# Seven products for eight on both pairs of output blocks of the down-projection, in four of its five portions

## The chip, the cores and the metric

The kernel runs on one core of one Trainium2 chip. The metric is the device time of one execution in microseconds (us): 2098.43 us is the median of three runs before the change (2096.87 to 2099.15). The core has a matrix engine (TensorE, PE in the profile, with PEld for loading its stationary operand), VectorE (DVE), ScalarE (ACT), GpSimd (POOL) and SyncE (SP), which here issues loads from HBM. Each engine works through its own list of instructions in order and waits on semaphores for the others.

## The reference

An encoder of two layers on 256 tokens of width 2048, in float32. Cut to what matters:

```python
for l in range(DEPTH):                      # DEPTH = 2
    h = rms_norm(x, ln1_g[l])
    qa, ka, va, qb, kb, vb = split(h @ w_in[l])
    oa = neighborhood_attention(...)        # 8 heads of 128, 2-D window
    ob = windowed_gqa_sink(...)             # 8 query heads, 2 key heads, band of +-128
    o = concatenate([rms_norm(oa, on_a[l]), rms_norm(ob, on_b[l])])
    x = x + o @ w_out[l]
    h2 = rms_norm(x, ln2_g[l])
    u = depthwise_conv(h2 @ w_up[l], conv_w[l], conv_b[l])   # 2048 -> 2 x 5632
    gate, up = u[..., :5632], u[..., 5632:]
    x = x + (silu(gate) * up) @ w_down[l]                    # 5632 -> 2048
```

The change concerns the last two lines, above all the product with w_down.

## The kernel before

**Precision.** Every weight that is multiplied is split into a rounded high part (ScalarE, line 114, tile `whi`) and the remainder (VectorE, line 115, tile `wlo`), 1024 columns at a time; activations are split in the same way. A product is then three matmuls: high by high, low by high, high by low. All of them are recorded under line 100, the helper `mm`.

**Quanta and steps.** The program is a list of quanta. A quantum is one load of 1024 KB of weights (tile `raw`, three buffers, issued on SP's queue at line 749 when the last split of the quantum three places earlier is done) and the matmuls that use it. It consists of two steps (three for a seven-product quantum, "seven"). While step s multiplies, the weights of step s + 4 are split (`SPLIT_AHEAD`), into five buffers each of `whi` and `wlo`. In every second quantum of an up block, the low part of the second half is not made by VectorE: seven steps ahead (`EARLY`) ScalarE writes the negated rounded weights into `v_a` or `v_b` (line 775), and a DMA on POOL's queue adds the raw weights to them (line 776). Which step is done so is decided by `by_transfer`.

**The feed-forward part.** The 5632 hidden columns are 44 blocks of 128. An up block f is two quanta, 64 matmuls; it accumulates in a PSUM tile "mm", of which there are two (two banks each), and `glu` (lines 544 to 570) reads it: a copy on ScalarE (548), an addition on VectorE (549) that is the last to read PSUM, the convolution (550 to 560), the gate (562, 564), and a split into the middle operand `mid`, which the down-projection uses as its stationary operand.

The down-projection goes in five portions (`CHUNKS`) of 8, 8, 8, 8 and 12 blocks. The 2048 output columns are four blocks of 512. For the first two of them, and pairs of hidden blocks, the four products of two token halves, two hidden blocks and two output blocks are done as seven products (a Strassen-like scheme) over four pairs: six of the seven in a seven-product quantum (`q_seven`, 18 matmuls of 512 columns in three steps), the seventh for all four pairs together in one "plain" quantum (`q_plain`, 12 matmuls). It needs sums of middle operands (`sums_mid`, once for every pair of blocks) and sums of weights, which VectorE forms in `raw` (lines 755 to 757, within `split_seven`). Six accumulators are open from the first of the four quanta to the last: one "mm" tile for two of them, both tiles "S", and "tr" and "pv". At the end `add_seven` adds them into `x` (lines 620 to 628). The last two output blocks go by ordinary quanta (`q_down`, 24 matmuls each), added to x on line 484.

**Order.** It is written out by hand at the end of `encoder_kernel`. In each layer nine up blocks come first; then each of the first four portions is: plain, four times a seven-product and an ordinary quantum, and eight up blocks of the next portion. The fifth portion is: plain, then seven-product quanta with the three remaining up blocks between them, then eight ordinary quanta. Splits of weights and `add_seven` have a higher scheduling priority than the rest (`AHEAD_PRIO`).

**Tiles.** Middle operands and operand sums are all tiles of the same size under the name "mid", 17 of them (`MIDS`); three further ones in the last portion use "qT" (`SPARE`), a tile of attention that is idle by then.

## Time and profile before

| what | value |
|---|---|
| median of the runs shown (range) | 2098.43 us (2096.87 to 2099.15) |
| the profiled execution | 2098.86 us |
| its span, first to last instruction | 2097.1 us |
| granted TensorE clock | 1.000 |
| weights read from HBM | 404.42 MB |

The profile is of one execution. A busy time is the time in which at least one instruction of the engine ran; a mean is the duration of one instruction, and neighbours overlap, so that means add up to more than busy time. Idle time is put down to the instruction or transfer that ended it ("<-"). Numbers such as L549 are lines of the kernel. The chain is followed back from the last instruction to whatever released each.

### The profile page before, as it was taken

How to read it: one execution, taken by the hardware profiler on the slowest of the kernel's cores; microseconds unless marked ns; L12 is line 12 of the kernel's file. 1: busy time of each engine (PE TensorE's matmuls, PEld its weight loads, DVE VectorE, ACT ScalarE, POOL GpSimd, SP SyncE). 2: the span in 40 equal slices, each digit the busy share in tenths (PEclk: the TensorE clock that was granted, in tenths of full speed). 3: DMA queues.
4: the chain of work that ended last, by engine and by line, in shares of the span. 5: the costliest groups of instructions: out<-in, count | busy, mean ns of one | idle time of the engine just before them, and what ended most of it. 6: DMA issues, size and time to landing. Idle time of an engine off the chain costs nothing.

```text
span 2097.1 us, 29473 instructions
## 1 busy us (share of the span) xinstructions
PE 2086.1 (99%) x10816; PEld 1787.8 (85%) x10816; DVE 1623.0 (77%) x2516; ACT 1308.8 (62%) x1905; POOL 241.5 (12%) x325
## 2 busy tenths in 40 slices
PE   9999999999999999999999999999999999999999
PEld 8888888888888888888888888888888888888887
DVE  7786656797887978788857766667978879788786
ACT  7566556766666666576555665567666666666663
POOL 0011101101101011020000111011011110111100
PEclk9999999999999999999999999999999999999999
DMA  9544557858678586787555455578686785867864
GB/s 351 196 145 166 175 181 213 242 204 252 206 253 267 206 258 201 229 272 230 208 181 181 161 169 171 165 220 248 209 256 206 243 254 210 270 199 240 262 211 161
DMA packets 74817, 454.57 MB, mean 217 GB/s; under 512 B 8752, under 2 KB 11312, under 8 KB 26416
## 3 DMA queue, kind: packets, MB, share of 16 engines
q1 hardware_dynamic: 61280, 405.46, 54.4%
q0 software_dynamic: 12672, 46.14, 12.3%
q8 instruction: 85, 1.39, 0.3%
q10 hardware_dynamic: 720, 1.08, 0.2%
q14 instruction: 60, 0.49, 0.1%
HBM read 404.42 MB, written 2.10 MB: 194 GB/s over the span
## 4 chain that ended last, share of the span: by engine, by line
PE 95%; DVE 2%; DMA 1%; issue 1%; ACT 1%; ACTq 0%; DVEq 0%; SPq 0%
PE mm L100 86%; PE S L100 3%; PE pv L100 2%; PE tr L100 1%; DVE wlo L115 1%; PE tr L375 1%; ACT whi L114 1%; PE tr L309 1%; PE S L151 0%; DMA v_a<-raw 0%; DMA mid<-in_xT 0%; DMA raw<-in_w_seven 0%; DMA raw<-in_w_up 0%; DVE pT L560 0%; DVE prob L549 0%
## 5 line engine op out<-in xcount | busy, mean ns | idle before, releaser
L115 DVE TENSOR_TENSOR wlo<-raw,whi 128x1024 fp32r<-128x1024 f32 (+1 forms) x709 | 858.2, 1221 | 298.2 <-ACT whi L114 265.8
L114 ACT ACTIVATE whi<-raw 128x1024 fp32r<-128x1024 f32 (+1 forms) x709 | 736.4, 1053 | 449.9 <-PE mm L100 220.7
L100 PE MATMUL mm<-xs,whi 128*128 128x512 f32 x2816 | 977.0, 390 | 3.0 <-DVE prob L549 3.0
L100 PEld LDWEIGHTS mm<-xs,whi 128*128 128x128 f32 x2816 | 527.8, 188 | 113.9 <-DVE prob L549 3.9
L100 PE MATMUL mm<-xs,wlo 128*128 128x256 f32 x2112 | 596.4, 282 | 0.6 <-DVE wlo L115 0.6
L100 PEld LDWEIGHTS mm<-xs,wlo 128*128 128x128 f32 x2112 | 399.1, 189 | 2.6 <-DVE wlo L115 1.5
L100 PE MATMUL mm<-whi,mid 128*128 128x512 f32 x1412 | 369.9, 392 | 1.6 <-DVE prob L549 1.2
L100 PEld LDWEIGHTS mm<-whi,mid 128*128 128x128 f32 x1412 | 262.5, 188 | 56.6 <-DVE prob L549 2.1
L100 PE MATMUL mm<-whi,xs 128*128 128x512 f32 x1152 | 294.7, 393 | 0.4 <-ACT whi L114 0.4
L100 PEld LDWEIGHTS mm<-whi,xs 128*128 128x128 f32 x1152 | 212.7, 188 | 43.1 <-ACT whi L114 1.4
L100 PE MATMUL mm<-wlo,mid 128*128 128x512 f32 x706 | 201.9, 392 | 0.0
L100 PE MATMUL mm<-wlo,xs 128*128 128x512 f32 x576 | 158.8, 392 | 0.0
L100 PEld LDWEIGHTS mm<-wlo,mid 128*128 128x128 f32 x706 | 132.2, 188 | 27.4
L560 DVE SCALAR_TENSOR_TENSOR pT<-halo,conv,pT 128x256 f32<-128x256 f32 x352 | 148.7, 481 | 6.5 <-ACT pT L558 1.6
L100 PEld LDWEIGHTS mm<-wlo,xs 128*128 128x128 f32 x576 | 107.0, 188 | 21.5
L552 POOL COPY halo<-halo 128x6 f32<-128x6 f32 x88 | 78.4, 891 | 352.8 <-DVE halo L550 352.8
L788 ACT ACTIVATE whi<-raw 128x1024 fp32r<-128x1024 f32 x88 | 92.7, 1053 | 40.1 <-PE mm L100 40.1
L558 ACT ACTIVATE pT<-halo,conv 128x256 f32<-128x256 f32 x176 | 96.0, 592 | 23.2 <-DVE halo L550 21.1
L100 PE MATMUL mm<-xs,v_a 128*128 128x256 f32 x352 | 99.3, 282 | 0.0
L100 PE MATMUL mm<-xs,v_b 128*128 128x256 f32 x352 | 99.2, 282 | 0.0
L776 POOL DMA_DIRECT2D v_b<-raw x44 | 38.1, 866 | 524.1 <-ACT v_b L775 299.6
L549 DVE TENSOR_TENSOR prob<-prob,mm 128x512 f32<-128x512 f32 x88 | 60.3, 685 | 46.9 <-ACT prob L548 46.9
(189 smaller groups left out, 1922.5 us busy)
## 6 DMA issues: line engine op xcount, KB each, us to landing
raw<-in_w_up SPq DMA_DIRECT2D x176, 1024.0 KB, 5.7
raw<-in_w_in SPq DMA_DIRECT2D x71, 1024.0 KB, 4.9
raw<-in_w_down SPq DMA_DIRECT2D x48, 1024.0 KB, 4.9
raw<-in_w_seven SPq DMA_DIRECT2D x40, 1024.0 KB, 5.1
raw<-in_w_out SPq DMA_DIRECT2D x32, 1024.0 KB, 4.8
v_a<-raw POOLq DMA_DIRECT2D x44, 512.0 KB, 5.5
v_b<-raw POOLq DMA_DIRECT2D x44, 512.0 KB, 5.1
raw<-in_w_plain SPq DMA_DIRECT2D x10, 1024.0 KB, 4.9
```

What stands on the lines that cost most here:

```text
L100: nc.tensor.matmul(ps, lhsT, rhs, start=start, stop=stop, skip_group_check=True)
L114: high = nc.scalar.activation(hi, src, AF.Copy)
L115: nc.vector.tensor_sub(lo, src, hi.bitcast(F32))
L309: nc.tensor.transpose(ps[:, j, tt * P:(tt + 1) * P], qn[tt][:, p + j, :], ident)
L375: nc.tensor.transpose(ps[:, kt, tt * P:(tt + 1) * P], p[:, tt, kt * P:(kt + 1) * P], ident)
L549: nc.vector.tensor_add(t, t, ps[:, :, 1])
L552: nc.gpsimd.tensor_copy(ux[:, :, 1:r], ux[:, :, T:T + r - 1])
L558: nc.scalar.activation(y[:, j, :], ux[:, j, r:r + T], AF.Identity, scale=w1, bias=b)
L560: nc.vector.scalar_tensor_tensor(y[:, j, :], ux[:, j, o:o + T], w, y[:, j, :], op0=ALU.mult, op1=ALU.add)
L776: nc.gpsimd.dma_start(out=lo, in_=src, accum_op=ALU.add)
L788: highs[s] = nc.scalar.activation(hl[s][0], raw[q][:, half * 1024:(half + 1) * 1024], AF.Copy)
```

## The change

- In the first four portions both pairs of output blocks go by seven products. `w_seven` and `w_plain` have one more index m for the pair, and `q_seven`, `q_plain` and `add_seven` take it. `q_down` remains for the fifth portion's second pair and remainder.
- The order in these portions is new: for each pair m a group of seven-product quantum 0, plain, seven-product 1, up, seven-product 2, up, seven-product 3, up, up. The eight up blocks of a portion thus stand within its two groups, and none is left ahead of the next portion.
- The operands of a portion live until its second group has used them. `middle` takes a tile from a table of names, MIDDLE: 17 "mid", and 3 "qT", 3 "qtok", 2 "kT" and 1 "kTb" of attention; `drop` gives a pair's names back.
- The second half of a plain quantum also has its low part made by ScalarE and a DMA.
- A few tiles have other widths (`ro`, `v_b`), and an 8-column tile `pad` is new.

```diff
@@ -53,7 +53,7 @@
 UP_AT = 56
 WARM = 14
 
-SPARE = 3 * (("qT", 3),)
+MIDDLE = (("mid", MIDS), ("qT", 3), ("qtok", 3), ("kT", 2), ("kTb", 1))
 
 EARLY = 7
 
@@ -171,7 +171,7 @@
         ps = psum.tile([P, TT], F32, name="pv", bufs=1)
         for tt in range(TT):
             mm(ps[:, tt:tt + 1], acc_o[grp][:, tt * P:(tt + 1) * P], ones[:, 0:1], True, True)
-        st["ro"] = act.tile([P, 16], F32, name="ro", bufs=2)[:, 0:TT]
+        st["ro"] = act.tile([P, TT], F32, name="ro", bufs=2)
         rsqrt(ps, 1.0 / (NH * HD), st["ro"], "c2")
 
 
@@ -267,6 +267,8 @@
 
     def evac_qk(ps, nh, kind):
 
+        if "pad" not in par:
+            par["pad"] = work.tile([P, 8], F32, name="pad", bufs=1)
         n = nh * HD
         grp, isq = kind[1], kind[0] == "q"
         qn = []
@@ -516,16 +518,23 @@
             at(q + 1, stat_x, which)
 
     gs = {}
-    count = {}
+    free, kept = {}, {}
 
     def middle(l, f):
 
-        name, bufs = "mid", MIDS
-        if f >= NF - CHUNKS[-1]:
-            k = count[l] = count.get(l, 0) + 1
-            if k > MIDS:
-                name, bufs = SPARE[k - MIDS - 1]
-        return act.tile([P, 2, T], F32R, name=name, bufs=bufs)
+        if f == 0 and l not in kept:
+            free.clear()
+            free.update(MIDDLE)
+            kept[l] = {}
+        name = max(free, key=lambda n: (free[n] > 0, n == "mid", free[n]))
+        assert free[name] > 0
+        free[name] -= 1
+        kept[l].setdefault(f // 2, []).append(name)
+        return (work if name == "qtok" else act).tile([P, 2, T], F32R, name=name, bufs=dict(MIDDLE)[name])
+
+    def drop(l, p):
+        for name in kept[l].pop(p):
+            free[name] += 1
 
     def q_up(l, f, u):
         def body(q, half, hi, lo):
@@ -584,7 +593,7 @@
             for j in range(2):
                 ss[p, 2 * i + j] = t[:, :, j * P:(j + 1) * P]
 
-    def q_seven(l, c, i):
+    def q_seven(l, c, m, i):
 
         f = sum(CHUNKS[:c]) + 2 * i
         p = f // 2
@@ -606,16 +615,20 @@
                 for x_part, w in ((0, hv), (1, hv), (0, lv)):
                     mm(ps[n], x2[:, x_part], w[:, j], i == 0 and x_part == 0 and w is hv,
                        i == PAIRS - 1 and w is lv)
-            if i == PAIRS - 1 and part == 2:
-                with tc.high_priority(offset=AHEAD_PRIO):
-                    add_seven(ps)
+            if part == 2:
+                if m == 1 and i > 0:
+                    drop(l, p)
+                if i == PAIRS - 1:
+                    with tc.high_priority(offset=AHEAD_PRIO):
+                        add_seven(m, ps)
         return body
 
-    def add_seven(ps):
+    def add_seven(m, ps):
 
         t = work.tile([P, 4, HD], F32, name="tq", bufs=2).rearrange("p a d -> p (a d)")
-        x11, x12 = x[:, 0, 0:512], x[:, 0, 512:1024]
-        x21, x_2, x2_ = x[:, 1, 0:512], x[:, :, 512:1024], x[:, 1, 0:1024].rearrange("p (j n) -> p j n", j=2)
+        xm = x[:, :, m * 1024:(m + 1) * 1024]
+        x11, x12 = xm[:, 0, 0:512], xm[:, 0, 512:1024]
+        x21, x_2, x2_ = xm[:, 1, 0:512], xm[:, :, 512:1024], xm[:, 1, 0:1024].rearrange("p (j n) -> p j n", j=2)
         both = lambda v: v[:, None, :].to_broadcast([P, 2, 512])
         nc.vector.tensor_add(x11, x11, ps[1])
         nc.scalar.activation(t, ps[1], AF.Copy)
@@ -639,7 +652,7 @@
             for tt in range(TT):
                 nc.sync.dma_start(out=out[:, tt, m], in_=x[:, tt, m])
 
-    def q_plain(l, c):
+    def q_plain(l, c, m):
 
         f0 = sum(CHUNKS[:c])
 
@@ -653,8 +666,10 @@
                     mm(ps, gs[f0 + 4 * half + 2 * i + 1][:, x_part, 0:P], w[:, i],
                        half == 0 and i == 0 and x_part == 0 and w is hv, half == 1 and i == 1 and w is lv)
             if half == 1:
-                xv = x[:, 0, 0:512]
+                xv = x[:, 0, m * 1024:m * 1024 + 512]
                 nc.vector.tensor_add(xv, xv, ps)
+                if m == 1:
+                    drop(l, f0 // 2)
         return body
 
     def q_down(l, c, nb, g):
@@ -711,18 +726,22 @@
         for c, nf in enumerate(CHUNKS):
             up = lambda f: [(a["w_up"][l, f, u], q_up(l, f, u), "up") for u in range(2)]
             down = lambda nb, g: [(a["w_down"][l, sum(CHUNKS[:c]) // FG + g, nb], q_down(l, c, nb, g), "")]
-            seven = lambda i: [(a["w_seven"][l, c, i], q_seven(l, c, i), "seven")]
-
-            end = sum(CHUNKS[:c]) + PART + 1
-            while f < end:
+            seven = lambda i, m=0: [(a["w_seven"][l, c, m, i], q_seven(l, c, m, i), "seven")]
+            plain = lambda m=0: [(a["w_plain"][l, c, m], q_plain(l, c, m), "plain")]
+
+            while f < PART + 1:
                 quanta += up(f)
                 f += 1
-            quanta.append((a["w_plain"][l, c], q_plain(l, c), ""))
             if nf == PART:
-                for i in range(PAIRS):
-                    quanta += seven(i) + down(2 + i // 2, i % 2)
+                for m in range(2):
+                    quanta += seven(0, m) + plain(m)
+                    for i in range(1, PAIRS + 1):
+                        if i < PAIRS:
+                            quanta += seven(i, m)
+                        quanta += up(f)
+                        f += 1
             else:
-
+                quanta += plain()
                 for i in range(PAIRS):
                     quanta += seven(i)
                     if f < NF:
@@ -762,14 +781,15 @@
 
     def by_transfer(s):
         q, half = steps[s]
-        return quanta[q][2] == "up" and half == 1 and last_up[q]
+        return half == 1 and (quanta[q][2] == "plain" or last_up.get(q, False))
 
     def low_w(s):
 
         if s < len(steps) and by_transfer(s):
             q, half = steps[s]
             src = raw[q][:, half * 1024:(half + 1) * 1024]
-            lo = lows[s] = act.tile([P, 1024], F32R, name=("v_a", "v_b")[turns[0] % 2], bufs=1)
+            n = turns[0] % 2
+            lo = lows[s] = act.tile([P, 1024 + 8 * n], F32R, name=("v_a", "v_b")[n], bufs=1)[:, 0:1024]
             turns[0] += 1
             with tc.high_priority(offset=AHEAD_PRIO):
                 nc.scalar.activation(lo, src, AF.Copy, scale=-1.0)
@@ -943,10 +963,10 @@
     wd = f["w_down"]
     n = NF // PART
 
-    four = wd[:, :n * PART * P, :1024].reshape(L, n, PART // 2, 2, P, 2, 512)
-    o["w_seven"] = c(np.stack([four[:, :, :, k, :, m] for k, m in ((1, 0), (1, 1), (0, 1), (0, 0))], 4)).reshape(
-        L, n, PART // 2, P, 2048)
-    o["w_plain"] = c(four[:, :, :, 1, :, 0].transpose(0, 1, 3, 2, 4)).reshape(L, n, P, 2048)
+    four = wd[:, :n * PART * P].reshape(L, n, PART // 2, 2, P, 2, 2, 512).transpose(0, 1, 5, 2, 3, 4, 6, 7)
+    o["w_seven"] = c(np.stack([four[:, :, :, :, k, :, m] for k, m in ((1, 0), (1, 1), (0, 1), (0, 0))], 5)).reshape(
+        L, n, 2, PART // 2, P, 2048)
+    o["w_plain"] = c(four[:, :, :, :, 1, :, 0].transpose(0, 1, 2, 4, 3, 5)).reshape(L, n, 2, P, 2048)
     o["w_down"] = c(f["w_down"].reshape(L, NF // FG, FG, P, NB, 512).transpose(0, 1, 4, 3, 2, 5)).reshape(
         L, NF // FG, NB, P, 2048)
```

## The prediction

> **What bounds the kernel now.** I read the engine totals and the chain that ended last first, then the chain in order of time, then windows over single stages.
>
> ```profile
> span 2097.1 us, 29473 instructions
> PE 2086.1 (99%) x10816; PEld 1787.8 (85%) x10816; DVE 1623.0 (77%) x2516; ACT 1308.8 (62%) x1905; POOL 241.5 (12%) x325
> PE 95%; DVE 2%; DMA 1%; issue 1%; ACT 1%; ACTq 0%; DVEq 0%; SPq 0%
> ```
>
> ```profile
> 467.27 94.69 PE mm L100 x538
> 596.86 94.69 PE mm L100 x538
> 726.46 94.69 PE mm L100 x538
> 856.05 84.21 PE mm L100 x480
> ...
> 1030.47 5.45 PE mm L100 x24
> ```
>
> TensorE (PE) is 95% of the chain. The chain repeats itself every 129.59 us (467.27, 596.86, 726.46, 856.05): that is one of the portions that the change edits, eight blocks of the up-projection ("ups") and then the down-projection of eight blocks. The last row gives the pace: 24 matmuls of 512 columns in 5.45 us, 0.227 us each. A "busy" mean of 390 ns for the same matmul counts overlapped time and is not used.
>
> ```profile
> core 0: us, PE busy (x) PEld busy (x) DVE busy (x) ACT busy (x) POOL busy (x), PEclk, DMA share, GB/s
> 467.27:596.86 129.59, 129.59 (x693) 112.44 (x693) 108.58 (x158) 84.12 (x111) 16.45 (x24) 1.00 0.74 235
> 856.05:944.30 88.25, 88.25 (x505) 77.94 (x505) 67.56 (x109) 59.20 (x82) 15.37 (x22) 1.00 0.84 256
> 948.52:1004.39 55.87, 53.08 (x279) 44.93 (x277) 45.53 (x62) 36.51 (x48) 3.60 (x9) 1.00 0.65 210
> 1993.25:2048.39 55.14, 53.08 (x278) 44.91 (x276) 45.65 (x62) 36.32 (x48) 3.61 (x9) 1.00 0.66 213
> 556.99:596.87 39.88, 39.88 (x182) 33.20 (x181) 39.56 (x48) 24.28 (x29) 1.17 (x2) 1.00 0.53 186
> ```
>
> In that portion PE has no gap, while VectorE (DVE) is busy 108.58 of 129.59 us. Eight ups take 88.25 us, 11.03 each. The two rows from 948.52 and from 1993.25 are the one place where the kernel already does what the change does everywhere: the fifth portion's first stretch, a plain product, then four seven-product steps with three ups between them. Only there does PE lose time: its work is 3 x 11.03 + (12 + 4 x 18) x 0.227 = 52.16 us, and it takes 55.87 and 55.14, a loss of 3.71 and 2.98.
>
> ```profile
> 956.10 0.38 PE L100 MATMUL mm<-xs,wlo 128*128 128x256 f32 x1 [0.37 <-DVE wlo L115]
> 988.27 0.50 PE L100 MATMUL mm<-xs,whi 128*128 128x512 f32 x1 [1.75 <-DVE prob L549]
> 1004.39 0.50 PE L100 MATMUL mm<-whi,mid 128*128 128x512 f32 x1 [0.67 <-DVE prob L549]
> 981.75 1.06 ACT L775 ACTIVATE v_b<-raw 128x1024 fp32r<-128x1024 f32 x1 [2.94 <-DMA raw<-in_w_up]
> 983.78 1.23 DVE L115 TENSOR_TENSOR wlo<-raw,whi 128x1024 fp32r<-128x1024 f32 x1 [2.99 <-ACT whi L114]
> ```
>
> How that loss arises: a load of weights is late by 2.94 us for ScalarE (ACT) at 981.75; DVE, which subtracts ACT's rounded part from the weights, idles 2.99 us behind it; DVE's addition on line 549, which frees the accumulator of the up before, comes late; PE waits 1.75 us at 988.27.
>
> **The change, part by part.** PE: a portion's second pair of output blocks took four ordinary steps of 24 matmuls, and takes four steps of 18 and a plain product of 12. That is 12 matmuls fewer, 12 x 0.227 = 2.72 us a portion; with four portions in each of two layers, 8 x 2.72 = 21.8 us. Nothing else is taken from PE, so this is all there is to win: 126.87 us a portion.
>
> [...]
>
> DVE, per portion:
>
> ```profile
> L115 DVE TENSOR_TENSOR wlo<-raw,whi 128x1024 fp32r<-128x1024 f32 x47 | 56.6, 1221 | 12.5 <-ACT whi L114 12.4
> L114 ACT ACTIVATE whi<-raw 128x1024 fp32r<-128x1024 f32 x46 | 47.4, 1052 | 23.4 <-DVE raw L755 9.1 <-DMA raw<-in_w_up 8.4 <-PE mm L100 2.4
> L755 DVE TENSOR_TENSOR raw<-raw 128x1024 f32<-128x1024 f32 x4 | 4.9, 1224 | 0.1
> L775 ACT ACTIVATE v_b<-raw 128x1024 fp32r<-128x1024 f32 x4 | 4.2, 1062 | 2.2 <-PE mm L100 1.4 <-DMA raw<-in_w_up 0.6
> L757 DVE TENSOR_TENSOR raw<-raw 128x512 f32<-128x512 f32 x4 | 2.8, 690 | 0.1
> L484 DVE TENSOR_TENSOR x<-x,mm 128x1024 f32<-128x1024 f32 x2 | 2.4, 1221 | 1.0 <-PE mm L100 1.0
> L625 DVE TENSOR_TENSOR x<-x,S 128x1024 f32<-128x1024 f32 x1 | 1.2, 1215 | 0.0
> L620 DVE TENSOR_TENSOR x<-x,mm 128x512 f32<-128x512 f32 x1 | 0.7, 687 | 0.2 <-PE mm L100 0.2
> ```
>
> Four more seven-product steps: 12 more subtractions of 1.221 (line 115), against 8 fewer of the ordinary steps; two plain products with one each, since their other half goes by DMA, where one had two. Net 4 x 1.221 = 4.9. Weight sums: 4 x (1.224 + 2 x 0.690) = 10.4. A second add_seven: two of 1.22 and six of 0.69, 6.6. A second plain addition 0.69, and two additions of line 484 fewer, -2.4. Together 20.1 us at the mean durations. These count the overlap of neighbours; where DVE runs without a break
>
> ```profile
> 591.01 5.93 DVE L115 TENSOR_TENSOR wlo<-raw,whi 128x1024 fp32r<-128x1024 f32 x5
> ...
> 597.13 0.69 DVE L620 TENSOR_TENSOR x<-x,mm 128x512 f32<-128x512 f32 x1 [0.19 <-PE mm L100]
> 597.73 1.22 DVE L115 TENSOR_TENSOR wlo<-raw,whi 128x1024 fp32r<-128x1024 f32 x1
> ```
>
> five take 5.93 and one of 0.69 makes way after 0.60; at that rate it is about 18. So DVE needs 108.6 + 18 to 20.1 = 126.6 to 128.7 us in a portion in which PE needs 126.87. The slack of 21 us is gone: DVE is level with PE.
>
> ACT: 6 more roundings of 1.052, 2 more of line 775 at 1.06 and one copy of 0.6 (nearest row: line 620, of the same size), 9.0 us: 93 of 126.9, beside PE's work. If ACT is held up, DVE has nothing to subtract, as at 983.78.
>
> DMA: 26 loads of weights on SP's queue for 25, and 10 accumulating transfers on POOL's for 8.
>
> ```profile
> raw<-in_w_up SPq DMA_DIRECT2D x176, 1024.0 KB, 5.7
> v_a<-raw POOLq DMA_DIRECT2D x44, 512.0 KB, 5.5
> ```
>
> There are three weight buffers, so behind an accumulating transfer (it reads the buffer) the next load into it starts only when that has landed: 5.5 + 5.7 us, and ACT's 1.06 ahead of them, 12.3 of the 15.1 us that an up and a seven-product step take (11.03 + 18 x 0.227). It fits by 3 us at the median; when loads crowd it does not, as at 981.75. In the plain product's case PE work from its split to the next wait on ACT (line 775, seven steps ahead) is one seven-product step and half a plain one, 5.4 us, against 5.7 to land: ACT is held by some 0.3 us, and up to 3 as in the row.
>
> Accumulators: four seven-product steps hold one of two "mm" tiles, both "S", "tr" and "pv". All ups of a group pass through the other "mm" tile, so each up waits until line 549 has read the up before; 4.1 us of PE work lie between. Before, that held for three ups of a layer; now for three in each of sixteen groups; the plain product waits so for the up ahead of the group, and the first up inside it for line 657.
>
> Costed at nothing: the middle operands in attention's tiles (17 tiles live at a portion's start, 25 of 26 at its middle; attention is over by then), the widths of ro, pad and v_b, the new order of w_seven and w_plain in HBM (still 1024 KB a load), the second pair's reuse of the operand sums (they exist). PE's 127 us a portion cover the first; if a tile were late, ACT would stand until the plain product is done, up to 6.8 us.
>
> **The sum.** The loss of the fifth portion's stretch, mean 3.35 us, is for four seven-product steps and three ups; a group has the four steps and four ups, so I take the same loss for each of a portion's two groups. Bounds: 0 (PE never waits, as in the portions now) and 4/3 of 3.71 = 4.95. I take 3.35 as the nearest row. A portion then takes 126.87 + 6.7 = 133.57 for 129.59, +3.98; eight of them +31.8. The profiled execution took 2098.86 us, 1.76 more than its span; the median of the runs is 2098.43. 2098.9 + 31.8 = 2131. Its own range is 2107 (only the stall of 988.27 recurs, 1.9 a group) to 2157.
>
> **Rivals.** *DVE packs, PE sets the end: faster.* The row 556.99:596.87 is the evidence: in the seven-product stretch of today's portions DVE is busy 39.56 of 39.88 us, and PE does not wait; work of ups that is left over fills every hole. Were DVE always so, a portion would take 126.87 (PE) to 128.7 / 0.992 = 129.7 (DVE), which is 2077 to 2100; I put it at 2086, a portion of 128.0. It holds while DVE's share stays over 98%. Against it: those 40 us start from a lead of four weight halves, have no accumulating transfers, and are followed by 88 us in which DVE catches up (67.56 of 88.25); after the change nothing follows.
> [...]
>
> *The two cancel.* A loss of 1.36 us a group gives back exactly the 2.72: 2099.
>
> *DVE as idle as in the fifth portion: much slower.* There it is busy 45.53 of 55.87, 81.5%. With 127.7 us of work that is 157 a portion, 2316; at 90%, 142 a portion, 2198. Against it: there it idles because it has too little work in hand, and leftovers would fill part.
>
> *The tiles don't hold what they are to hold.* If a group's middle operands wait for tiles, 1.4 to 6.8 us a portion come on top: 2142 to 2185.
>
> **How the numbers follow.** Forecast 0.41, packing 0.38, cancelling 0.10, much slower 0.08, late tiles 0.03. About 0.2%, 4 us, is what a measurement of this kernel can tell from no change. Faster 0.38; within it 0.10; slower 0.41 + 0.08 + 0.03 = 0.52. Range 2079 to 2165: it takes in nearly all of the packing case and the forecast's own 2107 to 2157, and leaves out most of the much slower one.
>
> **What would show it.** In the changed profile: the portion's period in the chain (133.6 forecast, 128.0 if DVE packs); x2 plain and x8 seven loads a portion; PE gaps before the first matmul of an up, released by DVE prob L549; ACT idle on DMA raw before line 775; DVE's share, 95% forecast, over 98% if it packs. A PE without such gaps makes the prediction wrong.

## The result, and the profile after

The changed kernel takes **2207.83 us** (median of three runs, 2206.13 to 2214.18) against 2098.43 before: a ratio of 1.053, with a 95% interval of 1.0496 to 1.0564. It is slower, as forecast, but by 109 us and not by 32, and outside the range of 2079 to 2165. The profiled execution took 2206.13 us, 1.8 more than its span.

The engine totals and the shares of the chain that ended last, from the page of the changed kernel:

```profile
span 2204.3 us, 29599 instructions
PE 2112.3 (96%) x10720; PEld 1791.2 (81%) x10720; DVE 1752.5 (80%) x2698; ACT 1366.9 (62%) x1979; POOL 240.2 (11%) x343
PE 63%; DVE 15%; DMA 11%; issue 7%; ACT 3%; POOL 1%; ACTq 0%; DVEq 0%; SPq 0%; POOLq 0%
```

TensorE held 95% of the chain before and holds 63% now; VectorE has 15% and DMA 11%. The windows of the changed kernel show the second portion, the fifth portion's first stretch, then two successive stretches inside the groups, and last the longer of these cut in two:

```profile
core 0: us, PE busy (x) PEld busy (x) DVE busy (x) ACT busy (x) POOL busy (x), PEclk, DMA share, GB/s
573.08:714.60 141.52, 132.68 (x682) 112.58 (x681) 123.28 (x179) 89.31 (x119) 15.71 (x26) 0.96 0.73 231
997.88:1060.30 62.42, 55.72 (x277) 47.09 (x276) 48.33 (x67) 37.50 (x50) 4.48 (x9) 0.95 0.68 213
659.57:692.30 32.73, 31.33 (x165) 26.88 (x163) 25.42 (x35) 20.20 (x26) 2.06 (x4) 0.97 0.75 236
692.30:731.73 39.43, 35.73 (x178) 29.82 (x179) 37.18 (x57) 25.10 (x36) 5.53 (x9) 0.94 0.72 217
692.30:714.60 22.30, 22.30 (x128) 19.77 (x129) 20.71 (x31) 12.80 (x19) 2.74 (x6) 1.00 0.85 259
714.60:731.73 17.13, 13.43 (x52) 10.06 (x51) 16.47 (x27) 12.30 (x18) 2.79 (x3) 0.85 0.55 163
```

A portion takes 141.52 us, where 126.87 is TensorE's work: 7.3 us are lost in each of its two groups. Inside a group the two halves, here called the light and the dense one, differ. (A "seven-product step" is here, as in the prediction, a whole seven-product quantum; a lead is counted in halves of a load, 1024 columns of weights each.) In the half of 31 to 33 us (an up, a seven-product step, an up, a step) VectorE is busy 25.4 us and waits. In the half of 38 to 39 us (two ups, step 0, the plain product, step 1, and beside them the additions of the seven sums) VectorE has 37 us of work, where TensorE alone would need 33.0 (2 x 11.03 + 48 x 0.227). The loss of the dense half lies at its end: the two ups take 22.30 us, nearly their pace, and the 48 matmuls of step 0, the plain product and step 1, worth 10.9 us, take 17.13, with VectorE busy 16.47 of them.

The chain of the changed kernel in order of time, through one group (columns: start us, us, what):

```profile
656.40 1.24 DVE wlo L115
657.65 4.95 DMA raw<-in_w_seven
...
668.87 1.07 ACT v_a L795
670.33 9.71 DMA v_a<-raw
680.18 4.84 DMA raw<-in_w_up
...
688.40 6.53 DMA raw<-in_w_up
...
704.47 1.14 DVE x L638
707.91 0.68 DVE prob L558
709.19 1.14 DVE raw L774
...
716.03 1.21 DVE wlo L115
...
727.47 1.07 ACT whi L114
728.58 1.22 PE pv L100 x2
```

Two things follow each other in a closed loop. From 657 to 695 the chain hangs mostly on loads: an accumulating transfer of 9.71 us, then the load that had to wait for its buffer. From 695 to 729 it hangs on VectorE: the additions of the seven sums, the up's addition, the weight sums (lines 774 to 776), the subtraction. A late subtraction lets the next load start late (656.40, 657.65), and it begins again. The waits over the whole span (columns: total us, times, longest us) name the same places; "S" and "pv" are accumulators of the seven products, so the last two are waits for the split weights of such a step:

```profile
ACT whi L114 <- DVE raw L774: 102.5, 62, 2.6
PE mm L100 <- DVE prob L558: 30.0, 15, 4.5
PE S L100 <- DVE wlo L115: 24.7, 14, 2.3
PE pv L100 <- ACT whi L114: 22.1, 16, 2.0
```

### The profile page after: what moved, and what is told of

The parts are those of the page before. It is cut to its first block, busy times and chain, and to the rows that moved or that the text cites. A ratio compares the mean times of both kernels' runs of the same rounds, so it can differ in the third digit from the quotient of the medians.

```text
span 2204.3 us, 29599 instructions
## 1 busy us (share of the span) xinstructions
PE 2112.3 (96%) x10720; PEld 1791.2 (81%) x10720; DVE 1752.5 (80%) x2698; ACT 1366.9 (62%) x1979; POOL 240.2 (11%) x343
## 4 chain that ended last, share of the span: by engine, by line
PE 63%; DVE 15%; DMA 11%; issue 7%; ACT 3%; POOL 1%; ACTq 0%; DVEq 0%; SPq 0%; POOLq 0%
PE mm L100 56%; DMA raw<-in_w_up 6%; DVE wlo L115 4%; ACT whi L114 3%; PE pv L100 3%; DVE pT L569 2%; PE S L100 2%; DMA raw<-in_w_seven 2%; DMA v_a<-raw 2%; DMA v_b<-raw 1%; POOL halo L561 1%; PE tr L100 1%; DVE raw L774 1%; DVE raw L776 1%; DVE halo L559 1%
## 5 line engine op out<-in xcount | busy, mean ns | idle before, releaser
L115 DVE TENSOR_TENSOR wlo<-raw,whi 128x1024 fp32r<-128x1024 f32 (+1 forms) x739 | 893.9, 1219 | 324.6 <-ACT whi L114 294.2
L114 ACT ACTIVATE whi<-raw 128x1024 fp32r<-128x1024 f32 (+1 forms) x739 | 770.3, 1054 | 526.7 <-PE mm L100 220.1
L100 PE MATMUL mm<-xs,whi 128*128 128x512 f32 x2816 | 996.4, 396 | 21.8 <-DVE prob L558 21.8
L100 PE MATMUL mm<-whi,mid 128*128 128x512 f32 x1024 | 286.0, 398 | 8.7 <-DVE prob L558 8.3
L100 PEld LDWEIGHTS mm<-whi,mid 128*128 128x128 f32 x1024 | 193.6, 191 | 49.8 <-DVE prob L558 9.1
L100 PE MATMUL mm<-wlo,mid 128*128 128x512 f32 x476 | 149.0, 396 | 0.0
L808 ACT ACTIVATE whi<-raw 128x1024 fp32r<-128x1024 f32 x106 | 111.4, 1051 | 23.1 <-PE mm L100 21.6
L561 POOL COPY halo<-halo 128x6 f32<-128x6 f32 x88 | 64.6, 734 | 398.7 <-DVE halo L559 398.7
L100 PEld LDWEIGHTS mm<-wlo,mid 128*128 128x128 f32 x476 | 90.1, 190 | 18.7
L796 POOL DMA_DIRECT2D v_a<-raw x53 | 46.2, 871 | 473.4 <-ACT v_a L795 365.4
```

Source lines behind the costliest of these rows:

```text
L100: nc.tensor.matmul(ps, lhsT, rhs, start=start, stop=stop, skip_group_check=True)
L114: high = nc.scalar.activation(hi, src, AF.Copy)
L115: nc.vector.tensor_sub(lo, src, hi.bitcast(F32))
L561: nc.gpsimd.tensor_copy(ux[:, :, 1:r], ux[:, :, T:T + r - 1])
L796: nc.gpsimd.dma_start(out=lo, in_=src, accum_op=ALU.add)
L808: highs[s] = nc.scalar.activation(hl[s][0], raw[q][:, half * 1024:(half + 1) * 1024], AF.Copy)
```

## The experiments

All are edits of the changed kernel but the last. Each is one execution, with the kernel before run beside it (2097.0 to 2100.2 us), so it has no interval; only the last has one. The changed kernel's own three runs span 8 us (2206.13 to 2214.18), so less than that says little. "Loss" is the time above TensorE's bound, which the first experiment shows to be about 2077 us.

**The weight sums left out.** The three sums of lines 774 to 776 are not made, so the products use the loaded weights.

```diff
         if part == 1:
-            nc.vector.tensor_sub(w[:, 1:3], w[:, 1:3], w[:, 2:4])
-            nc.vector.tensor_add(w[:, 3], w[:, 3], w[:, 1])
-            nc.vector.tensor_sub(w[:, 0], w[:, 3], w[:, 0])
+            pass
```

> Leaves out the sums of weights in the seven-product steps (three VectorE instructions each, lines 774 to 776), so the products use unsummed weights. Theory A, VectorE is overloaded (124 us of work in a portion of 142 us, bunched around the first two steps of a group): VectorE has 19 to 21 us less a portion, the period falls from 142 to 127 to 130 us, the time to 2095 to 2115 us, and the granted clock returns to 1.00. Theory B, loads that come late behind accumulating transfers and three weight buffers hold ScalarE, and VectorE idles for it: the loads stay, the period stays at 139 us or more, the time at 2185 us or more. Theory C, the single accumulator that the ups share makes PE wait for line 558: between the two, 2150 to 2185 us.

2076.55 us, 23.7 below the kernel before. Its first portion, and one dense half of a group, in the windows:

```profile
430.10:557.61 127.51, 127.33 (x683) 110.09 (x682) 106.31 (x156) 90.83 (x119) 17.42 (x26) 1.00 0.82 255
663.49:696.60 33.11, 33.11 (x178) 28.69 (x177) 30.59 (x49) 25.45 (x35) 6.33 (x9) 1.00 0.74 236
```

TensorE sets the end: 127.51 against 126.87, with all the accumulating transfers and the single accumulator in place. The dense half needs 30.59 us of VectorE in 33.11 and keeps pace. So the whole loss of 130 us goes when 94 us a layer of VectorE's work go.

**No accumulating transfers.** The transfer of line 796 is dropped, so these halves keep a wrong low part.

```diff
                 nc.scalar.activation(lo, src, AF.Copy, scale=-1.0)
-                nc.gpsimd.dma_start(out=lo, in_=src, accum_op=ALU.add)
```

> Leaves out the accumulating transfers: ScalarE still writes the negated rounded weights into v_a and v_b, and the raw weights are not added to them, so these low parts are wrong. All of the 106 transfers of 512 KB go. Theory A (VectorE overloaded): VectorE has as much to do as before, 2190 to 2207 us. Theory B (late loads): a weight buffer is free 5 to 9 us earlier, loads land in 5 us, the period falls from 142 to 130 to 133 us, the time to 2110 to 2140 us. Theory C: 2190 us or more.

2155.97 us, between the theories' ranges: 50 of the 130 go. The same pair of half groups in its windows:

```profile
647.34:677.59 30.25, 30.25 (x163) 26.19 (x164) 26.13 (x35) 20.80 (x27) 0.31 (x2) 1.00 0.65 240
677.59:715.74 38.15, 35.35 (x178) 29.77 (x178) 37.15 (x57) 25.26 (x35) 2.54 (x6) 0.95 0.49 170
```

The light half is at TensorE's pace, while the dense one still takes 38.15 us with VectorE busy 37.15. The late loads cost in the first. In the second, with loads on time, VectorE has hardly a gap: it is busy 22.17 of 22.21 us in the two ups and 14.98 of 15.94 in the 48 matmuls behind them.

**The additions of the seven sums left out.** Only the first of the nine operations stays, so seven of a group's eight additions into `x` are left out.

```diff
         nc.vector.tensor_add(x11, x11, ps[1])
-        nc.scalar.activation(t, ps[1], AF.Copy)
-        nc.vector.tensor_add(t, t, ps[6])
...
-        nc.vector.tensor_sub(x21, x21, ps[4])
```

> Leaves out seven of the eight additions with which add_seven brings the products into x, and ScalarE's copy there; x gets one product alone. VectorE has 5.3 us less a group, 10.6 a portion, in no chain that a matmul waits for soon. Theory A (the amount): about half of what leaving out the weight sums brought (2207 to 2077), 2120 to 2155 us. Theory D (the chain of the sums): 2195 to 2207 us.

2175.34 us, 31 less, again between the ranges.

```profile
498.57:636.96 138.39, 129.65 (x682) 109.41 (x681) 115.09 (x168) 89.53 (x118) 13.97 (x26) 1.00 0.76 236
684.97:723.00 38.03, 36.06 (x179) 30.15 (x180) 31.68 (x50) 24.76 (x35) 5.01 (x9) 0.96 0.77 225
```

VectorE is busy 115.09 of 138.39 us, 83%, and the dense half holds 31.68 us of its work: nearly the 30.59 of the first experiment, which ran at 33.11 and lost nothing. So VectorE's amount in a half group does not decide alone: at nearly the same amount the half with the weight sums loses 5 us and the half with the additions nothing. Most of the difference lies in the 48 matmuls, which take 14.2 us here and 10.92 in the first experiment.

**Both left out**, transfers and additions, to see whether they are two causes or one:

```diff
-        nc.scalar.activation(t, ps[1], AF.Copy)
...
-        nc.vector.tensor_sub(x21, x21, ps[4])
...
-                nc.gpsimd.dma_start(out=lo, in_=src, accum_op=ALU.add)
```

> Leaves out both the accumulating transfers and seven of the eight additions of add_seven (what each leaves out is as in the two runs that leave out one of them; those took 2156 and 2175 us, where the changed kernel took 2207). If the loads' lateness and VectorE's amount each cost their own time, the gains add up: 51 + 32, 2124 us. If late loads only take away VectorE time that it could do without, were its work less, then with loads on time 10.6 us less a portion is enough to end PE's waits: 2080 to 2095 us.

2131.43 us: the two gains add (50 + 31 = 81 expected from single runs, 75 measured). Some 55 us of loss are left with both gone, 3.4 us a group. A dense half, its two ups and then its 48 matmuls:

```profile
678.29:700.48 22.19, 22.19 (x129) 19.66 (x128) 18.15 (x27) 13.98 (x18) 1.96 (x4) 1.00 0.56 193
700.48:714.54 14.06, 11.92 (x51) 8.86 (x49) 13.18 (x25) 10.63 (x16) 1.39 (x2) 1.00 0.44 153
```

In this half all that is left lies in the 48 matmuls: VectorE is busy 13.18 us there, where TensorE's work is 10.9, though it idles for 4 of the 22.19 us ahead of them.

**The weight sums left out of the second pair alone:**

```diff
-        if part == 1:
+        if part == 1 and m == 0:
```

> Leaves out the weight sums of the second pair of output blocks alone (products there use unsummed weights): 10 us of VectorE work less a portion, half of what leaving out all of them takes away. Theory A2 (the amount decides, wherever it lies): as without add_seven, which takes away as much elsewhere, 2165 to 2185 us. If the place decides: every second group runs free, half of the 130 us come back, 2135 to 2150 us.

2142.68 us: half of the 130 stay. Three groups in its windows, without, with and without the sums:

```profile
633.75:698.06 64.31, 63.76 (x343) 55.10 (x341) 53.72 (x80) 45.09 (x60) 7.91 (x13) 1.00 0.78 245
698.06:768.80 70.74, 67.15 (x342) 57.15 (x341) 61.62 (x89) 45.93 (x61) 7.75 (x13) 0.95 0.75 236
768.80:832.90 64.10, 63.76 (x343) 55.09 (x341) 54.91 (x82) 45.25 (x60) 7.84 (x13) 1.00 0.79 249
```

A group with the sums loses 7 us though the one ahead lost nothing, and the next is back at pace at once. The loss is made inside the group that has the work, not carried in.

**The same amount elsewhere.** The sums are left out, and the multiplication of an up's output is repeated instead: VectorE's amount is that of the changed kernel, but no weight waits for it.

```diff
-            nc.vector.tensor_sub(w[:, 1:3], w[:, 1:3], w[:, 2:4])
...
-        nc.vector.tensor_mul(ux[:, :, r:r + T], t, st["r2"][:, None, :].to_broadcast([P, 2, T]))
+        for _ in range(5 if PART < f + 1 < NF else 1):
+            nc.vector.tensor_mul(ux[:, :, r:r + T], t, st["r2"][:, None, :].to_broadcast([P, 2, T]))
```

> The three weight sums are left out (the output is then not the reference's), and the multiplication of line 559 is done five times instead of once in the 35 ups of a layer that lie beside seven-product steps. VectorE's extra work is 35 x 4 x 0.684 = 95.8 us a layer, the sums were 36 x (1.22 + 2 x 0.69) = 93.6: the amount stays that of the changed kernel, but it stands behind an up, and no rounding of weights waits for its data. If the amount of VectorE's work a group decides: 2195 to 2215, group near 71 us. If the place inside the weights' chain decides: 2077 to 2105, group near 64 to 65 us, with VectorE about 97% busy in the portions.

2179.76 us: 103 of the 130 come back, below the range named for the amount and far above that for the place. The windows of the two parts of a portion, from one addition of a plain product to the next, and three waits over the span:

```profile
580.00:646.30 66.30, 65.79 (x340) 56.78 (x340) 56.39 (x81) 43.28 (x55) 7.99 (x11) 0.96 0.67 208
646.30:720.70 74.40, 65.92 (x343) 55.77 (x342) 69.81 (x114) 50.15 (x69) 14.14 (x15) 0.96 0.79 246
```

```profile
PE mm L100 <- ACT mid L114: 51.8, 8, 7.5
PE tr L100 <- ACT whi L114: 10.2, 10, 2.6
PE mm L100 <- DVE prob L558: 9.3, 9, 2.8
```

TensorE's three waits shown above for the changed kernel (77 us) shrink to 9.3, beside 10.2 on "tr", and a new one of 51.8 us is there: once a portion TensorE waits up to 7.5 us for a middle operand, which in the chain hangs behind the repeated multiplications. So about half of what came back is a wait that the experiment itself made. Neither theory holds alone; these waits read as if, with VectorE this full, whichever chain gets the work comes late.

**The same place without the data chain.** The sums are replaced by two products of a constant, 2.44 us for 2.60, written to the tile that the subtraction then overwrites; ScalarE's rounding need not wait for them.

```diff
-            nc.vector.tensor_sub(w[:, 1:3], w[:, 1:3], w[:, 2:4])
-            nc.vector.tensor_add(w[:, 3], w[:, 3], w[:, 1])
-            nc.vector.tensor_sub(w[:, 0], w[:, 3], w[:, 0])
+            r2 = st["r2"][:, None, :].to_broadcast([P, 4, T])
+            for _ in range(2):
+                nc.vector.tensor_mul(lo.rearrange("p (k n) -> p k n", k=4), r2, r2)
```

> The three weight sums are replaced by two products of 1024 columns of a constant, written to the tile that the following subtraction overwrites (the output is then not the reference's). 2 x 1.22 = 2.44 us for 2.60, at the same place of VectorE's queue, but they don't read the loaded weights, so ScalarE's rounding needn't wait for them. If the data chain load, sums, rounding, subtraction is what costs: 2080 to 2115. If it is only that VectorE is busy there, at that place: 2190 to 2206, group near 70 us. In between, both count, in proportion.

2169.95 us: between the two theories, 93 of the 130 come back with 94% of the amount. Waits of this run:

```profile
PE mm L100 <- DVE prob L558: 19.3, 18, 2.2
PE mm L100 <- DVE x L670: 19.2, 16, 2.0
PE mm L100 <- DVE mid L115: 16.7, 8, 3.1
PE S L100 <- DVE wlo L115: 2.3, 6, 1.0
```

TensorE's waits on "S" and "pv" are nearly gone (46.8 us in the changed kernel, 2.3 here), those on whatever else VectorE makes are there. VectorE's time at that place is thus enough for 93 of the 130 us without the data chain. But two of the waits shown (19.2 and 16.7 us) are not in the changed kernel, so the rest, 36 us, is not the price of the data chain: the two can't be parted by this run.

**The sums in a tile of their own**, off the data chain but reading the loaded weights, with one score tile fewer to make room:

```diff
+            d = work.tile([P, 512], F32, name="aside", bufs=1)
+            nc.vector.tensor_sub(d, w[:, 1], w[:, 2])
...
-    for i in range(3):
+    for i in range(2):
```

> Keeps the VectorE time of the weight sums and takes away what hangs on them: four VectorE instructions of 512 columns write the differences into a tile of their own, which nothing reads, and the products use unsummed weights (one of three attention score tiles is given up for the room). Theory A (the amount of VectorE work): as after the change, 2190 to 2220 us. Theory D (the chain load, sums on VectorE, rounding on ScalarE, subtraction on VectorE is too long, and ScalarE waits in it for lines 774 and 776): as without the sums, 2077 to 2110 us.

2225.49 us, and inconclusive. The first sum now stands ahead of any wait on ScalarE, so VectorE itself waits for the load:

```profile
DVE aside L775 <- DMA raw<-in_w_seven: 45.9, 24, 5.3
```

**GpSimd as a helper.** First the weight sums on GpSimd, then, in another kernel, line 559 and the sums of the middles (lines 586 to 589):

```diff
-            nc.vector.tensor_sub(w[:, 1:3], w[:, 1:3], w[:, 2:4])
+            nc.gpsimd.tensor_sub(w[:, 1:3], w[:, 1:3], w[:, 2:4])
...
```

> The three sums of weights of a seven-product step are made by GpSimd and not by VectorE; the result is the reference's. VectorE has 19 to 21 us less a portion. Theory A (the amount of VectorE work): 2077 to 2120 us, if GpSimd's three sums take up to 10 us of the 15 us that an up and a seven-product step last. Theory D (the chain): it gets longer by GpSimd's slower additions, 2210 us or more.

```diff
-        nc.vector.tensor_mul(ux[:, :, r:r + T], t, st["r2"][:, None, :].to_broadcast([P, 2, T]))
+        nc.gpsimd.tensor_mul(ux[:, :, r:r + T], t, st["r2"][:, None, :].to_broadcast([P, 2, T]))
...
-        nc.vector.tensor_add(v[:, 0], m1[:, b], m2[:, b])
+        nc.gpsimd.tensor_add(v[:, 0], m1[:, b], m2[:, b])
```

> Line 559 (the scaling into the halo tile) and the four sums of middle operands go to GpSimd; the result is the reference's. VectorE has 8 x 0.61 + 16 x 0.3 = 9.7 us less a portion. Theory A: 2125 to 2160 us. Theory D: 2195 us or more, since the chain of the weight sums is as it was.

2392.54 and 2225.09 us. A group of instructions of the first (columns: busy us, mean ns of one, idle before and its cause), then groups of the second:

```profile
L774 POOL TENSOR_TENSOR raw<-raw 128x1024 f32<-128x1024 f32 x72 | 180.8, 2512 | 240.7 <-DVE wlo L115 239.3 <-issue 1.3
```

```profile
L559 POOL TENSOR_TENSOR halo<-prob,acc_b 128x512 f32<-128x512 f32 x88 | 143.8, 1634 | 138.8 <-DVE prob L558 138.5
L115 DVE TENSOR_TENSOR wlo<-raw,whi 128x1024 fp32r<-128x1024 f32 x737 | 930.1, 1276 | 337.1 <-ACT whi L114 302.2 <-PE mm L100 25.6 <-ACT mid L117 3.8
L775 DVE TENSOR_TENSOR raw<-raw 128x512 f32<-128x512 f32 x72 | 62.2, 864 | 1.0
```

GpSimd takes 2512 ns for what VectorE does in 1218 in the changed kernel (line 774), in the chain of the weights, and its queue, which also issues the accumulating transfers, stands 239 us waiting for VectorE. Off that chain the time grows too, and VectorE's own operations are longer than in the changed kernel (1219 ns for line 115, 685 for line 775).

**Smaller undoings.** The plain product's low half by VectorE again; the even order of steps and ups; that with no accumulating transfers; the up's accumulator read first; loads issued later:

```diff
-        return half == 1 and (quanta[q][2] == "plain" or last_up.get(q, False))
+        return half == 1 and last_up.get(q, False)
```

> Undoes one part of the change: the second half of a plain quantum is split by VectorE again, 18 accumulating transfers fewer, 18 subtractions of 1.22 us more. Theory A (VectorE overloaded): 1.2 us more a group, 2215 to 2230 us. Theory B (late loads): the next up's load no longer waits for that transfer, 2170 to 2195 us. Theory C: no change, 2200 to 2212 us.

```diff
-                    for i in range(1, PAIRS + 1):
-                        if i < PAIRS:
+                    for i in range(PAIRS):
+                        if i > 0:
```

> The same work in another order: a group is seven-product step 0, plain, up, step 1, up, step 2, up, step 3, up, so that no two seven-product steps stand together and no two ups. Theory A (VectorE overloaded where step 0, plain and step 1 follow each other): the bunch is spread, the 5 us that PE loses there shrink to 1 to 3 us a group, 2130 to 2165 us. Theory B (late loads): as many loads at the same mean rate, 2190 to 2210 us. Theory C: four waits for an up's accumulator a group in place of three, 2200 us or more.

```diff
-                    for i in range(1, PAIRS + 1):
-                        if i < PAIRS:
+                    for i in range(PAIRS):
+                        if i > 0:
...
-                nc.gpsimd.dma_start(out=lo, in_=src, accum_op=ALU.add)
```

> Leaves out the accumulating transfers (low parts of these steps are wrong, as in the run without them) and uses the even order: step 0, plain, up, step 1, up, step 2, up, step 3, up. Without the transfers alone the time was 2156 us, and what PE still lost lay where step 0, plain and step 1 follow each other (13.8 us for 10.9). Theory A1, VectorE's work is too bunched there: spread out, the loss goes, 2090 to 2120 us. Theory A2, VectorE's work is too much for the portion wherever it lies: 2145 to 2165 us.

```diff
-        nc.scalar.activation(t, ps[:, :, 0], AF.Copy)
-        nc.vector.tensor_add(t, t, ps[:, :, 1])
+        with tc.high_priority(offset=3 * AHEAD_PRIO):
+            nc.scalar.activation(t, ps[:, :, 0], AF.Copy)
+            nc.vector.tensor_add(t, t, ps[:, :, 1])
```

> Gives the two instructions that free an up's accumulator (lines 557 and 558) a higher scheduling priority than the splits of weights; the result is the reference's. Theory C (the single accumulator of the ups): PE's 30 us of waits for line 558 go, and what follows from them, 2150 to 2185 us. Theory A (VectorE's amount): the splits come later by as much, 2195 to 2220 us.

```diff
-EARLY = 7
+EARLY = 5
```

> ScalarE's part of a split by transfer comes five steps ahead and not seven; the result is the reference's. Theory B (late loads hold ScalarE ahead of its other work): ScalarE stands less ahead of line 795, 2170 to 2195 us, unless the transfers then land too late for PE. Theory A: 2200 us or more, since VectorE's work is the same.

In this order 2217.21, 2206.13, 2163.19, 2202.40 and 2208.86 us. With VectorE's subtraction in place of the plain product's transfer the kernel is 11 us slower in this one run, so the transfer there was no cause. The order of ups and steps, the priority of the accumulator's two reads and the time of the issue move the total by 7 us at most, which single runs do not tell from nothing. None of them alone sets the loss. In the even order no two seven-product steps stand together, and the loss stays: TensorE waits 44.5 us for line 558 and 31.2 for line 635 instead.

**One more half of lead.** Five weight halves ahead instead of four, paid for with one score tile instead of three, two "pT" tiles instead of four, and narrower padding; beside it a control with the same cuts and the old lead. With one score tile a head's scores are overwritten by the next head's before they are transposed, so attention there computes something else; the amount of work stays.

```diff
-SPLIT_AHEAD = 4
+SPLIT_AHEAD = 5
...
-        y = work.tile([P, 2, T], F32, name="pT", bufs=4)
+        y = work.tile([P, 2, T], F32, name="pT", bufs=2)
...
-    for i in range(3):
+    for i in range(1):
```

> Weights are split five steps ahead and not four, with six buffers each of whi and wlo; the room comes from attention's tiles (one score tile for three, two pT for four) and 32 bytes less a buffer. The result is the reference's. Theory A3 (the lead of four steps is too short: VectorE has slack in the ups that it cannot use for the weight sums and splits of the steps of 1.36 us that follow, so the loss is local to the groups that have the sums): a group falls from 71 to 66 to 69 us against the control with the same cuts, 30 to 80 us in all. Theory A2 (the amount alone, or late loads): a group within 1 us of the control's.

```diff
-    for i in range(3):
+    for i in range(1):
```

> The control: the same cuts in attention's tiles and in the buffers' width, with the lead of four steps; the result is the reference's. Attention may lose some us; a group of the down-projection should stay at 70 to 72 us, the time at 2205 to 2235 us, under every theory.

2270.92 us against the control's 2249.40. The one wait that grew, first with five halves, then in the control:

```profile
PE mm L100 <- DVE prob L558: 73.1, 33, 4.3
```

```profile
PE mm L100 <- DVE prob L558: 36.4, 18, 4.2
```

TensorE's waits on "S" and "pv" shrink from 47 to 15 us. The reading is that more room to prepare weights ahead lets their subtractions take VectorE's queue before the addition that frees an up's accumulator: the wait is moved, and the total grows. Five halves together with that addition put first was not run.

**The accumulator read first, in the kernel before**, the edit that had come out lowest among those that leave nothing out (by 4 us, less than the runs differ) and could be put there:

```diff
-        nc.scalar.activation(t, ps[:, :, 0], AF.Copy)
-        nc.vector.tensor_add(t, t, ps[:, :, 1])
+        with tc.high_priority(offset=3 * AHEAD_PRIO):
+            nc.scalar.activation(t, ps[:, :, 0], AF.Copy)
+            nc.vector.tensor_add(t, t, ps[:, :, 1])
```

> The kernel before with the same higher priority for lines 548 and 549; the result is the reference's. PE waited 1.75, 0.67 and about 2 us more in the other layer for line 549 in the fifth portion. If the priority is the cause of these waits, 2094 to 2096 us, 0.1 to 0.2% faster than before; if VectorE is late there for other reasons (loads), within 1 us of before.

2098.26 us (median of 11 runs), a ratio of 1.0001 with an interval of 0.9992 to 1.001: no difference. No version that computes all of the reference and beats the kernel before was found.

## Why the prediction was right and wrong

**TensorE's gain: right, the close total in part by luck.** Without the weight sums a portion takes 127.4 to 128.1 us where 126.87 was worked out. The kernel gains 23.7 us where 21.8 was, but only some 15 of them come from the portions; the fifth portion's first stretch, at 52.41 us for 55.87 and 55.14 before, gives 6 that the sum did not have.

**The work of VectorE and ScalarE: nearly right.** Busy 123 to 125 and 89 to 91 us a portion, 126.6 to 128.7 and 93 forecast. "Level with TensorE" was the right reading, and the waits forecast are there: the first matmul of an up on line 558 (30.0 us), ScalarE on loads ahead of line 795 (46.2 and 46.0 us on those of the ups).

**The size of the loss: wrong, and this is the step that failed.** "A group has the four steps and four ups, so I take the same loss for each": 3.35 us, with 4.95 as the upper bound. A group loses 7.3 to 8 us. Three things broke the step.

- The row was not a price of a group's code. In the fifth portion's first stretch an up stands between any two seven-product steps; in a group step 0, the plain product and step 1 follow each other. Nor was it a price of its own code: where the plain product's low half is VectorE's again, that stretch is as in the kernel before, and it takes 58.32 and 60.38 us for 55.87 and 55.14, behind a group, whose additions fall into it, and not behind eight ups. In the changed kernel it takes 62.42; with neither those additions nor any accumulating transfer it took 52.42.
- VectorE's slack over a portion does not reach the stretch that needs it. The prediction added up a portion, found the two engines level, and took the mean for a price. In the changed kernel 48 matmuls worth 10.9 us take 17.13, with VectorE busy 16.47, while it idles 5.5 to 7 us in the light half. More of TensorE's waits are for the weights of such steps (46.8 us on "S" and "pv") than for line 558 (30.0), which is the wait that was forecast. These 48 matmuls are where the loss shows, not shown to be why it is there: the even order breaks them up and loses as much. The prediction had the chance of VectorE being 10% idle at 0.08, with 142 us a portion and 2198 as its price; 141.5 and 2208 came.
- The margin of 3 us for a load behind an accumulating transfer was counted at median durations, 5.5 and 5.7 us. In the chain the transfer takes 9.71 and the load behind it 4.84, so the 15.1 us are used up. Without these transfers 50 us go.

The three causes that single runs show (130, 50 and 31 us) sum to more than the loss of 130: they are not shares of it. Taking any of them away gives VectorE or the loads slack, and the others then cost less. What the runs show is that VectorE's added work is needed for the loss: without the weight sums it goes whole, and with the same amount of work elsewhere 103 us come back, about half of them in a wait that the changed kernel does not have. How it divides between the amount and the place is open. Two rivals fall: VectorE did not pack (123.28 of 141.52 us is 87%, not 98%), and the two effects did not cancel. The tiles of attention were no cost: TensorE has no wait on a middle operand among its rows in the changed kernel.

**Not settled:** why VectorE cannot use its idle 5.5 to 7 us in the light half. By the chain it waits there for ScalarE, ScalarE for loads, and those for buffers which VectorE's late work holds; but without the accumulating transfers, where the light half is at pace, the dense half still takes 38 us. A longer lead with the up's addition kept ahead of it may be the way; no run shows it.

## What to carry to other kernels

Where a change takes work from the engine that bounds and fills a second engine to the same level, compare the two over stretches as short as the buffers between them can bridge, not over the whole period, nor over half of it. Here the dense half with 37 us of VectorE's work for 33.0 of TensorE's looks like the cause, but with 31.68 us it took nearly as long; the 48 matmuls, with weights made ready four halves ahead, told more. A stall taken from a stretch in which the helper still had slack was less than half of what the same steps cost without it (3.35 us, against 7.3 to 8 in a group). Count a chain of transfers at the durations that it has while loads crowd, not at their medians (here 9.71 us, against 5.2 to 5.7).

## What the runs showed of the hardware that was not expected

**The clock fell beside the stalls.** The prediction took one pace for TensorE. The view of the cores gives the changed kernel a mean granted clock of 0.981, where the windows of the kernel before read 1.00; a window of the changed kernel and the timeline of TensorE around its start (the bracket holds the idle time before the instruction and its cause):

```profile
core 0: 2204.3 us, clock 0.981
```

```profile
654.90:661.80 6.90, 5.53 (x16) 4.41 (x16) 5.89 (x8) 5.15 (x6) 0.00 (x0) 0.51 0.87 235
```

```profile
654.31 0.50 PE L100 MATMUL S<-wlo,qtok 128*128 128x512 f32 x1 [1.86 <-DVE wlo L115]
...
656.42 1.22 PE L100 MATMUL pv<-whi,kT 128*128 128x512 f32 x2 [1.37 <-ACT whi L114]
...
658.72 0.63 PE L100 MATMUL pv<-wlo,kT 128*128 128x512 f32 x1
659.14 0.63 PE L100 MATMUL mm<-wlo,qT 128*128 128x512 f32 x1
```

Behind the wait of 1.86 us the clock is still 1.00 up to 654.9; from 655.0 on it is 0.50, so the wait of 1.37 us already falls in the slow stretch, which lasts 6.8 us (to 661.75). Matmuls of 512 columns start 0.42 us apart there (658.72, 659.14), where 0.227 is the pace. Other such stretches last 3.4 us (477.43 to 480.85, at 0.50). Each of the 18 in this trace begins during a wait of TensorE or within 1.1 us of the end of one. 0.019 x 2204 = 42 us of full-speed time is the most that this can have cost; it is part of the loss above, not beside it, since without the weight sums the clock is 1.00. The rows of what TensorE waited for in the changed kernel sum to 86 us (30.0, 24.7 and 22.1 above, and 5.9, 2.0 and 1.6); with the 42 they make up nearly all of the 130. So a wait cost twice here: as itself, and as slow matmuls behind it.

A single wait of 1.86 us, with matmuls on both sides of it, went ahead of the fall at 655; in the kernel before, the row from 948.52 to 1004.39 holds a wait of 1.75 us, and its clock is 1.00. What makes the clock fall these runs do not show.

**VectorE was slower beside GpSimd.** With about 144 us of line 559 on GpSimd, and the sums of the middles, VectorE's subtraction of 1024 columns went from a mean of 1219 ns, as the page of the changed kernel has it, to 1276, and the weight sum of 512 columns on line 775 from 685 to 864; the one on line 776 stayed at 685. With the weight sums on GpSimd the subtraction took 1255.

```profile
L115 DVE TENSOR_TENSOR wlo<-raw,whi 128x1024 fp32r<-128x1024 f32 (+1 forms) x739 | 893.9, 1219 | 324.6 <-ACT whi L114 294.2
```

**An accumulating transfer of 512 KB stretched.** Its median is 5.1 to 5.7 us in the two kernels, but 9.71 us in the chain (670.33), where two loads of 1024 KB of weights were issued at 670.20 and 673.94.
